# Row sums of the later modulations with the data as stationary operand, and the context norm's squares two steps earlier

## The chip, the cores and the metric

The kernel runs on one core of one Trainium2 chip. The metric is device time in microseconds (us) from one launch, the median over a few runs; lower is better. The core has five engines that run side by side and wait for each other by semaphores: TensorE (PE; its loads of stationary operands are listed apart as PEld), VectorE (DVE), ScalarE (ACT), GpSimd (POOL) and SyncE (SP), which here issues nearly all DMA transfers from one queue.

## The reference

One layer of a diffusion backbone over 1024 latent tokens and 256 context tokens, model width 1024, all in f32. Each sub-layer's input is normed and modulated by a shift and a scale, and its output scaled by a gate; these nine vectors ("modulations", m = 0 to 8) come from one product each for latents and context:

```
mod_lat = silu(c) @ w_mod + b_mod        # (1024) @ (1024 x 9*1024)
mod_ctx = silu(c_ctx) @ w_mod + b_mod
ml, mc = split(mod_lat, 9), split(mod_ctx, 9)
x  = x  + 0.5*ml[2]*swiglu(modulate(rms_norm(x,  norm1_g), ml[0], ml[1]), ffn1_w_in, ffn1_w_out)
cx = cx + 0.5*mc[2]*swiglu(modulate(rms_norm(cx, norm1_g), mc[0], mc[1]), ffn1_w_in, ffn1_w_out)
hx = modulate(rms_norm(x,  norm2_g), ml[3], ml[4])
hc = modulate(rms_norm(cx, norm2_g), mc[3], mc[4])
...  # hx, hc @ w_in: gated short convolution and grouped-query attention, merged
x = x + ml[5]*merge(...)
x = x + 0.5*ml[8]*swiglu(modulate(rms_norm(x, norm3_g), ml[6], ml[7]), ffn2_w_in, ffn2_w_out)
return rms_norm(x, final_g)
```

Context modulations above m = 4 are not needed, since the layer is the last.

## The kernel before

Activations lie transposed, channels on the 128 partitions and tokens along the free axis. PE's large products take each operand as two parts: a high part, the f32 number cast to a format that PE reads in one pass (`F32R`), and a low part, the difference (`split`: a cast on ACT, a subtraction on DVE). A product is three matmuls of parts. The FFN products (`Winograd`, `row_products`) use a fast scheme over 2 x 2 blocks with seven products instead of eight. Their inputs are loaded into `raw` tiles, added in part on POOL (`s`, `sum`), split into `wl` and fed to PE.

The first two modulations for the latents come from functions of their own at the start. All others are `later_mod`. It works in halves of 512 columns. For a half, eight tiles `rawm` (128 x 512) of `w_mod` are loaded, and DVE multiplies each by the 128 numbers of silu(c), one for each partition, and adds it into an accumulator `macc`, one accumulator for each stream (latents v = 0, context v = 1). What is left is a sum over the 128 partitions, for 512 columns, and it has to end with the 512 results laid out as 128 partitions x 4, in `modl` or `modc`, with the bias `bcol` added. The old way to do it is: split the accumulator into `acch` and `accl`; two matmuls with a column of ones (`ones_r`) as the stationary operand and 512 moving columns, which give one row of 512 sums in PSUM; a copy of the row on ACT that also reorders it (`mrow`); a DMA of 2 KB from that row into a 128 x 4 tile (`mcol`); an add on DVE.

There are 17 halves and 23 sums: three halves for the context alone (second half of m = 1, both of m = 0), six with both streams (m = 2, 3, 4), eight for the latents alone (m = 5 to 8).

`later_mod` is a generator. Each `yield` ends a step, and `run(steps, n)` in other loops takes n steps at a place, so that this work is issued between rounds of other products. A half takes 19 steps before: eight with a load and multiply-adds, four empty (`WAIT`), then the split and six steps, then the matmuls, copy, transfer and add, in step 19. Where steps are taken:

- First FFN, loop over 22 column blocks j: six steps at the end of each of j = 1 to 12 (`STEPS`), none at 13. Each of these j holds five to seven products of twelve matmuls. These 72 steps begin with the three context halves, then the first context norm `modulated_norm` (normc), then m = 2. After j = 13 come 14 rounds of context products with two steps each (`BATCH`), then 11 steps at the end of each j from 14 on. All that is left over is taken at once behind the loop.
- The mixing products, loop over i = 0 to 7: two steps of the second context norm (normc2) after a first group of seven products; from i = 3 on also eight steps of m = 5. One or two further groups follow in each i.
- The value projection over ten token tiles: three steps of m = 6 and 7 after each; then five after each group of heads. Here the weights are loaded four at a time (`by_four`).
- Second FFN: three steps of m = 8 after each j from 2 on.

`modulated_norm` for the 256 context tokens squares on ACT and adds on DVE (`sum_squares`, result `sq_acc`), ends the step, sums over the partitions on PE with `rstd_cols`, whose products already have the data stationary and the f32 column `ones` moving, computes 1/sqrt on DVE in eleven small operations (`rs_a`, `rs_y`, `rs_t`), waits four steps and then scales the channels, one in each step.

Order on the engines: the program is written for a scheduler that plans each engine's order from a model of costs. It may put instructions that it takes to be ready ahead of those issued earlier, except that one marked `pinned` stays behind the instruction issued just before it on its engine. Each engine then runs its list in order and waits at its head for whatever it needs. SP's queue does likewise: a transfer that waits for its data holds back every load behind it. Tiles come from pools with a fixed number of buffers: small working tiles (`ttile`: `rawm`, `macc`, `acch`, `accl`, `mrow`, `s1` to `s3`, `sq` and others) share eleven, and `ps_t` in PSUM has two.

Of the kernel before, what the change touches and what calls it, by code (L numbers as in the profile page):

```python
# [10 lines left out]
F32R = mybir.dt.float32r  # L11
# [7 lines left out]
P = 128  # L19
# [32 lines left out]
def tile_dit_layer(  # L52
# [44 lines left out]
    act, dve, pool, pe, sp = (Engine(e) for e in (nc.scalar, nc.vector, nc.gpsimd, nc.tensor, nc.sync))  # L97
# [11 lines left out]
    def uniq(s):  # L109
        n_tiles[0] += 1  # L110
        return f"{s}_{n_tiles[0]}"
# [4 lines left out]
    def ttile(name, n=512, dt=F32):  # L116
        t = tpool.tile([P, 512], dt, tag="t", name=uniq(name))
        return t[:, :n]

    def small(name, n, dt=F32):  # L120
        return spool.tile([P, n], dt, tag=f"s{n}_{name}", name=uniq(name))
# [4 lines left out]
    def ps_t(n=512):  # L126
        return psum.tile([P, 512], F32, tag="t", name=uniq("pt"), bufs=2)[:, :n]
# [4 lines left out]
    def matmul(out, w, x, start, stop, pinned=False, on=False):  # L132

        inst = pe.matmul(out, w, x, start=start, stop=stop, skip_group_check=on)
        if pinned:
            tc.keep_in_program_order(inst)
# [7 lines left out]
    def load(out, in_, pinned=False):  # L144
        inst = sp.dma_start(out=out, in_=in_)
        if pinned:
            tc.keep_in_program_order(inst)
# [4 lines left out]
    ones = const.tile([P, 1], F32, name="ones")  # L152
    dve.memset(ones[:], 1.0)
    ones_r = const.tile([P, 1], F32R, name="ones_r")
# [4 lines left out]
    bcol = const.tile([P, 72], F32, name="bcol")  # L159
# [26 lines left out]
    def col(name, k=0):  # L186
        o = voff[name] + k
        return cols[:, o : o + 1]
# [4 lines left out]
    modl = const.tile([P, 72], F32, name="modl")  # L193
    modc = const.tile([P, 40], F32, name="modc")


    def split(src, hi, lo, lo_eng=None, hi_eng=None):

        if hi_eng is dve:
            dve.tensor_copy(out=hi, in_=src)  # L200
        else:
            act.copy(out=hi, in_=src)
        (lo_eng or dve).tensor_sub(out=lo, in0=src, in1=hi.bitcast(F32))
# [47 lines left out]
    def rstd_cols(accs, n, dim):  # L251

        nt = n // P
        pss = ps_t(nt)
        for j in range(nt):
            for i, acc in enumerate(accs):
                matmul(
                    pss[:, j : j + 1], acc[:, j * P : (j + 1) * P], ones[:], start=(i == 0),
                    stop=(i == len(accs) - 1), pinned=True,
                )  # L260
        a = small("rs_a", nt)
        dve.tensor_scalar(out=a[:], in0=pss, scalar1=dim * EPS, scalar2=None, op0=ALU.add)
        return rsqrt_cols(a[:], nt)

    def bcast(y, n):

        pr = ps_t(n)
        for j in range(n // P):
            transpose(pr[:, j * P : (j + 1) * P], y[:, j : j + 1].to_broadcast([P, P]), pinned=True)
        return pr  # L270

    def later_mod(m, halves=(0, 1), streams=None, by_four=False):

        if streams is None:
            streams = (0, 1) if m < 5 else (0,)
        for half in halves:
            raws = fetch_mod(m, half, False) if by_four else None
            accs = [ttile(f"macc{v}") for v in streams]
            o = m * D + half * 512
            for k in range(KD):  # L280
                if by_four:
                    raw = raws[k // 2][:, k % 2]
                else:
                    raw = ttile("rawm")
                    load(out=raw, in_=w_mod[0, k * P : (k + 1) * P, o : o + 512])
                for acc, v in zip(accs, streams):
                    s = silu_c[:, v * 8 + k : v * 8 + k + 1]
                    if k == 0:
                        dve.tensor_scalar(out=acc, in0=raw, scalar1=s, scalar2=None, op0=ALU.mult)
                    else:  # L290
                        dve.scalar_tensor_tensor(out=acc, in0=raw, scalar=s, in1=acc, op0=ALU.mult, op1=ALU.add)
                yield
            for _ in range(WAIT):
                yield
            parts = []
            for acc in accs:
                ah, al = ttile("acch", dt=F32R), ttile("accl", dt=F32R)
                split(acc, ah, al)
                parts.append((ah, al))
            for _ in range(6):  # L300
                yield
            for (ah, al), v in zip(parts, streams):
                mod, pm = (modl, modc)[v], ps_t()
                matmul(pm[:1], ones_r[:], ah, start=True, stop=False, pinned=True)
                matmul(pm[:1], ones_r[:], al, start=False, stop=True, pinned=True)
                row = ttile("mrow")
                act.copy(
                    out=row[:1].rearrange("o (p j) -> o j p", j=4), in_=pm[:1].rearrange("o (j p) -> o j p", j=4)
                )
                mcol = small("mcol", 4)  # L310
                sp.dma_start(out=mcol[:], in_=row[:1])
                c0 = m * 8 + half * 4
                dve.tensor_add(out=mod[:, c0 : c0 + 4], in0=mcol[:], in1=bcol[:, c0 : c0 + 4])
            yield

    def fetch_mod(m, half, pinned=True):
        raws = []
        for kk in range(KD // 2):
            raw = atile("rawm", (P, 2, 512))
            o = m * D + half * 512  # L320
            load(raw[:], w_mod[0, kk * 256 : (kk + 1) * 256, o : o + 512].rearrange("(a p) n -> p a n", p=P), pinned)
            raws.append(raw)
        return raws
# [106 lines left out]
    def sum_squares(xs, ch):  # L430
        n = ch[2]
        acc, acc2 = ttile("sq_acc", n), ttile("sq_acc2", n)
        for k in range(KD):
            sq = (acc, acc2)[k] if k < 2 else ttile("sq", n)
            act.activation(out=sq, in_=xs(k, ch), func=AF.Square)
            if k >= 2:
                a = (acc, acc2)[k % 2]
                dve.tensor_add(out=a, in0=a, in1=sq)
        dve.tensor_add(out=acc, in0=acc, in1=acc2)
        return acc  # L440

    def modulated_norm(xs, hh, hl, ch, gain, mod, m):

        s, o, n = ch
        acc = sum_squares(xs, ch)
        yield
        y = rstd_cols([acc], n, D)
        for _ in range(WAIT):
            yield
        pr = bcast(y, n)  # L450
        for k in range(KD):
            if k:
                yield
            t = ttile("nt", n)
            dve.tensor_mul(out=t, in0=xs(k, ch), in1=pr)
            dve.tensor_scalar(
                out=t, in0=t, scalar1=gain[s][:, k : k + 1], scalar2=mod[s][:, m * 8 + k : m * 8 + k + 1],
                op0=ALU.mult, op1=ALU.add,
            )
            split(t, hh(k, ch), hl(k, ch))  # L460
        yield
# [613 lines left out]
    for k in range(4):  # L1075
        if k % 2:
            half1.shifted(h0[k][:, 0], k, xh[k])
        else:
            dve.tensor_scalar(
                out=h0[k][:, 0], in0=xh[k], scalar1=gain1["l"][:, k : k + 1], scalar2=modl[:, k : k + 1],  # L1080
# [3 lines left out]
    start = half1.start_by_half()  # L1084
# [44 lines left out]
    for i in range(2):  # L1129
        sp.dma_start(out=cxd[i], in_=xc.t[i][:].rearrange("p a b -> p (a b)"))  # L1130
    hc = Context("h1ch", F32R), Context("h1cl", F32R)
    normc = modulated_norm(xc, *hc, CC, gain1, mods, 0)

    def all_later_mods():
        yield from later_mod(1, (1,), (1,))
        yield from later_mod(0, (0, 1), (1,))
        part_gain(gain1["c"], 0, "g1", "c", 0, 8)
        for _ in normc:
            yield
        for m in range(2, 5):  # L1140
            yield from later_mod(m)
# [68 lines left out]
    for j in range(NH):  # L1210
        half1.side = side(j) if j >= SIDE_FROM else None
        u, c = half1.next_first()
        v, b = half1.second(u)
# [25 lines left out]
    for d in range(0, KD, 2):  # L1239
# [8 lines left out]
        for e in range(2):  # L1248
            te = t[:, e * CT : (e + 1) * CT]
            dve.scalar_tensor_tensor(  # L1250
                out=te, in0=pt[:, e * CT : (e + 1) * CT], scalar=gate1["c"][:, d + e : d + e + 1], in1=te, op0=ALU.mult, op1=ALU.add
# [78 lines left out]
    for i in range(KD):  # L1330
# [6 lines left out]
        for ch, bg, gc in mixed():  # L1337
            gate(gcd, i, ch, gc)
            o = ch[1]
            y = ttile("y")  # L1340
            dve.tensor_scalar(out=y, in0=u[:, o : o + 512], scalar1=col("w1", i), scalar2=None, op0=ALU.mult)
            for j in (0, 2):
# [3 lines left out]
                    out=ya, in0=u[:, a + j - 1 : b + j - 1], scalar=col(f"w{j}", i), in1=ya, op0=ALU.mult, op1=ALU.add  # L1346
# [42 lines left out]
    for kt in range(10):  # L1389
        ch = CC if kt < 2 else C0 if kt < 6 else C1  # L1390
        o = (kt if kt < 2 else (kt - 2) % 4) * P
# [327 lines left out]
    for ch in (C0, C1):  # L1719
        o = ch[1]  # L1720
        for d in range(KD):
# [7 lines left out]
                out=xs(d, ch), in0=ps, scalar=modl[:, 40 + d : 41 + d], in1=xs(d, ch), op0=ALU.mult, op1=ALU.add  # L1729
# [12 lines left out]
        out=gf[:], in0=cols[:, voff["gf"] : voff["gf"] + 8], scalar1=math.sqrt(D), scalar2=None, op0=ALU.mult  # L1742
# [46 lines left out]
    for j in range(NH):  # L1789
# [3 lines left out]
        v, b = fast.second(u)  # L1793
# [81 lines left out]
```

## Time and profile before

| | |
|---|---|
| median of three runs | 2670.65 us (2669.2 to 2675.72) |
| the profiled execution | 2670.08 us, span 2668.3 us |
| PE | busy 2633.8 us, 99% of the span |
| DVE | 2002.0 us, 75% |
| ACT | 1173.6 us, 44% |
| POOL | 558.4 us, 21% |
| mean granted PE clock | 0.996 |

The span runs from the first to the last instruction; the execution's own time has some 2 us around it. Matmuls overlap in PE's pipeline: a duration in a row is longer than the distance to the next start, so PE's price of an instruction is read from start to start. In a time line, a bracket at a row's end is the idle time of the engine before it and what ended that. In a table of stretches the columns are the length, the busy time of each engine asked for with its number of instructions, the granted PE clock, the DMA share and GB/s. The row of a tile gives the shortest, median and longest duration in ns. All matmul and vector lines carry the line number 90, that of the helper which issues them, so tiles tell the groups apart.

### The profile page before, as it was taken

Reading aid. Unit: us, or ns where it says so; the run is one execution under the profiler, and the core shown is the slowest. Engines: PE = TensorE matmul, PEld = TensorE weight load, DVE = VectorE, ACT = ScalarE, POOL = GpSimd, SP = SyncE. Lnnn points to the kernel's source line nnn. Section 1 sums busy time; section 2 is a strip of 40 time slices with the busy share of each in tenths; the row PEclk is TensorE's granted clock in tenths of the full one; section 3 lists DMA queues with packets and bytes.
Section 4 is the critical chain, followed back from the end, with each engine's and each line's share of the span. In section 5 each row is a group of like instructions: output and inputs, shape, how many; then the busy total and the mean of one; then the engine's idle time right before and its main releaser. Section 6 shows DMA issues by size and latency. Waiting matters only on the chain.

```text
span 2668.3 us, 36840 instructions
## 1 busy us (share of the span) xinstructions
PE 2633.8 (99%) x13373; PEld 2220.0 (83%) x13373; DVE 2002.0 (75%) x3356; ACT 1173.6 (44%) x2317; POOL 558.4 (21%) x449
## 2 busy tenths in 40 slices
PE   8999999999999999999999999999999999999998
PEld 6787799888778878888999888888888888888888
DVE  5788976788887899877598676685458976657885
ACT  6532454333454643333355576574236333334443
POOL 0134301111020034332033122141001532330200
PEclk9999999999999999999999999999999999999999
DMA  8566475345984355342522432113525643227841
GB/s 320 194 194 189 138 230 158 115 131 187 302 206 119 126 179 173 98 134 72 202 68 92 91 95 62 35 41 98 167 87 171 196 146 97 86 88 285 188 90 64
DMA packets 371471, 381.12 MB, mean 143 GB/s; under 512 B 19526, under 2 KB 258264, under 8 KB 371288
## 3 DMA queue, kind: packets, MB, share of 16 engines
q1 hardware_dynamic: 360472, 357.22, 41.4%
q0 software_dynamic: 10816, 21.53, 4.9%
q8 instruction: 105, 1.72, 0.3%
q14 instruction: 78, 0.64, 0.1%
HBM read 308.88 MB, written 69.76 MB: 142 GB/s over the span
## 4 chain that ended last, share of the span: by engine, by line
PE 90%; DVE 5%; DMA 2%; issue 1%; ACT 1%; POOL 1%; SPq 0%; DVEq 0%; POOLq 0%; ACTq 0%
PE ps L90 74%; PE po L90 8%; PE pt L90 8%; DVE wl L90 1%; DVE r L90 1%; DMA raw<-in_ffn_w_in_dram 1%; DVE nt L90 0%; DMA rawm<-in_w_mod_dram 0%; DMA ws<-in_ffn_w_out_dram 0%; DVE u L90 0%; DVE macc L90 0%; POOL s L90 0%; DVE y L90 0%; POOL sum L90 0%; DVE sq_acc L90 0%
## 5 line engine op out<-in xcount | busy, mean ns | idle before, releaser
L90 PE MATMUL ps<-r,wl 128*128 128x512 f32 x5196 | 1206.8, 391 | 9.6 <-DVE wl L90 3.1
L90 PEld LDWEIGHTS ps<-r,wl 128*128 128x128 f32 x5196 | 974.4, 189 | 218.8 <-DVE wl L90 5.9
L90 ACT CAST wl<-raw 128x512 fp32r<-128x512 f32 x287 | 177.7, 620 | 229.8 <-PE ps L90 173.3
L90 DVE TENSOR_TENSOR wl<-raw,wl 128x512 fp32r<-128x512 f32 x287 | 202.3, 706 | 60.6 <-ACT wl L90 56.7
L90 ACT CAST wl<-sum 128x512 fp32r<-128x512 f32 x168 | 103.2, 620 | 231.9 <-PE ps L90 184.9
L90 DVE TENSOR_TENSOR wl<-sum,wl 128x512 fp32r<-128x512 f32 x168 | 152.2, 908 | 17.8 <-ACT wl L90 16.8
L90 POOL TENSOR_TENSOR sum<-raw 128x512 f32<-128x512 f32 x42 | 60.6, 1443 | 497.9 <-DMA raw<-in_w_in_dram 203.2
L90 DVE SCALAR_TENSOR_TENSOR macc<-rawm,silu_c,macc 128x512 f32<-128x512 f32 x178 | 148.0, 849 | 13.5 <-DMA rawm<-in_w_mod_dram 12.8
L90 DVE TENSOR_TENSOR u<-u,ps 128x512 f32<-128x512 f32 x186 | 126.2, 680 | 33.6 <-PE ps L90 33.6
L90 PE MATMUL ps<-wh,r 128*128 128x256 f32 x768 | 141.6, 284 | 0.0
L90 DVE TENSOR_TENSOR pts<-pt,pts 128x512 fp32r<-128x512 f32 x160 | 108.7, 687 | 41.1 <-ACT pts L90 39.3
L90 ACT CAST pts<-pt 128x512 fp32r<-128x512 f32 x160 | 93.3, 595 | 86.4 <-PE pt L90 82.7
L90 DVE TENSOR_REDUCE m<-ps 128x1 f32<-128x512 f32 (+1 forms) x192 | 110.3, 595 | 23.9 <-PE ps L90 22.3
L90 ACT CAST rh<-hid 128x512 fp32r<-128x512 f32 x132 | 81.3, 620 | 104.6 <-PE ps L90 91.6
L90 PE MATMUL ps<-rh,wl 128*128 128x512 f32 x360 | 122.0, 389 | 0.0
L90 PEld LDWEIGHTS ps<-wh,r 128*128 128x128 f32 x768 | 120.8, 192 | 0.7 <-issue 0.6
L90 POOL TENSOR_TENSOR sum<-raw,sum 128x512 f32<-128x512 f32 x42 | 62.0, 1476 | 268.7 <-DVE wl L90 261.8
L90 ACT CAST wh<-raw 128x512 fp32r<-128x512 f32 (+1 forms) x85 | 67.9, 801 | 103.2 <-PE ps L90 70.2
L90 POOL TENSOR_TENSOR s<-raw 128x512 f32<-128x512 f32 x22 | 32.0, 1457 | 378.5 <-DMA raw<-in_ffn_w_in_dram 297.1
L90 PE MATMUL po<-pts,vh 128*128 128x512 f32 x256 | 110.0, 435 | 0.2 <-ACT pts L90 0.2
L90 PE MATMUL ps<-wl,r 128*128 128x256 f32 x384 | 109.0, 284 | 0.0
L90 DVE TENSOR_TENSOR rl<-hid,rh 128x512 fp32r<-128x512 f32 x132 | 90.3, 686 | 21.7 <-PE ps L90 11.7
(317 smaller groups left out, 5382.9 us busy)
## 6 DMA issues: line engine op xcount, KB each, us to landing
raw<-in_ffn_w_in_dram SPq DMA_DIRECT2D x130, 512.0 KB
raw<-in_ffn_w_out_dram SPq DMA_DIRECT2D x72, 512.0 KB
raw<-in_w_in_dram SPq DMA_DIRECT2D x61, 512.0 KB
rawm<-in_w_mod_dram SPq DMA_DIRECT2D x104, 256.0 KB
hid<-hd SPq DMA_DIRECT2D x40, 512.0 KB
rawm<-in_w_mod_dram SPq DMA_DIRECT2D x32, 512.0 KB
ws<-in_ffn_w_out_dram POOLq DMA_DIRECT2D x30, 512.0 KB, 6.5
ucd<-uc SPq DMA_DIRECT2D x29, 512.0 KB
```

Source lines behind the costliest of these rows:

```text
L90: inst = getattr(self.engine, name)(*args, **kw)
```

## The change

In `later_mod` the split, the two matmuls over 512 columns, the row copy and the transfer go. Each accumulator, as it is (f32), becomes the stationary operand in four products of 128 x 128, with the f32 column `ones` moving. Each gives 128 sums, one on each partition, in one column of a PSUM tile `pm`; both streams share one tile. DVE adds the bias from PSUM into `modl` or `modc`. The sum is issued in step 13 of a half, right after the four empty steps, and four steps follow: a half has 16 steps. In `modulated_norm` the sum of squares is followed by three step ends instead of one.

```diff
             for _ in range(WAIT):
                 yield
-            parts = []
-            for acc in accs:
-                ah, al = ttile("acch", dt=F32R), ttile("accl", dt=F32R)
-                split(acc, ah, al)
-                parts.append((ah, al))
-            for _ in range(6):
+            pm = ps_t(4 * len(streams))
+            for i, acc in enumerate(accs):
+                for j in range(4):
+                    matmul(
+                        pm[:, 4 * i + j : 4 * i + j + 1], acc[:, j * P : (j + 1) * P], ones[:], start=True, stop=True,
+                        pinned=True,
+                    )
+            c0 = m * 8 + half * 4
+            for i, v in enumerate(streams):
+                dve.tensor_add(
+                    out=(modl, modc)[v][:, c0 : c0 + 4], in0=pm[:, 4 * i : 4 * i + 4], in1=bcol[:, c0 : c0 + 4]
+                )
+            for _ in range(4):
                 yield
-            for (ah, al), v in zip(parts, streams):
-                mod, pm = (modl, modc)[v], ps_t()
-                matmul(pm[:1], ones_r[:], ah, start=True, stop=False, pinned=True)
-                matmul(pm[:1], ones_r[:], al, start=False, stop=True, pinned=True)
-                row = ttile("mrow")
-                act.copy(
-                    out=row[:1].rearrange("o (p j) -> o j p", j=4), in_=pm[:1].rearrange("o (j p) -> o j p", j=4)
-                )
-                mcol = small("mcol", 4)
-                sp.dma_start(out=mcol[:], in_=row[:1])
-                c0 = m * 8 + half * 4
-                dve.tensor_add(out=mod[:, c0 : c0 + 4], in0=mcol[:], in1=bcol[:, c0 : c0 + 4])
-            yield
...
         acc = sum_squares(xs, ch)
-        yield
+        for _ in range(3):
+            yield
         y = rstd_cols([acc], n, D)
```

## The prediction

> **What bounds the kernel now.** I read the page first (busy shares, then the chain that ended last), then the tiles of the sums that the change touches, then the time line of TensorE (PE) around them, and last the waits and the clock.
>
> ```profile
> span 2668.3 us, 36840 instructions
> ...
> PE 2633.8 (99%) x13373; PEld 2220.0 (83%) x13373; DVE 2002.0 (75%) x3356; ACT 1173.6 (44%) x2317; POOL 558.4 (21%) x449
> ...
> PE 90%; DVE 5%; DMA 2%; issue 1%; ACT 1%; POOL 1%; SPq 0%; DVEq 0%; POOLq 0%; ACTq 0%
> ```
>
> PE is busy for 99% of the span and carries 90% of the chain. So each microsecond put into PE's stream lengthens the program nearly one for one, and what other engines save is worth only the PE idle time that it ends. The stretches in which the later modulations run show how little of that there is:
>
> ```profile
> 200.00:270.00 70.00, 66.72 (x285) 1.00 0.59 183
> ...
> 330.00:690.00 360.00, 360.00 (x2088) 1.00 0.54 176
> ```
> ```profile
> 1330.00:1460.00 130.00, 130.00 (x1039) 127.03 (x1038) 114.24 (x299) 64.14 (x218) 41.79 (x80) 1.00 0.23 74
> 2080.00:2300.00 220.00, 220.00 (x972) 181.71 (x971) 163.10 (x221) 70.47 (x116) 80.90 (x56) 1.00 0.44 135
> ```
>
> The columns are length, then PE busy. PE is idle for 3.3 us between 200 and 270, and for nothing from 330 to 690, from 1330 to 1460 and from 2080 to 2300, where 19 of the 23 sums are.
>
> **The sums on PE, old and new.** The rows of the old sums and of the row-sum products that already have the new form (f32 data stationary, a column of ones moving):
>
> ```profile
> L90 PE MATMUL pt<-acch,ones_r x23: 388/397/400, 192.6 to 2280.6; 128*1 128x512 f32 x23
> ...
> L90 PE MATMUL pt<-accl,ones_r x23: 389/397/398, 192.9 to 2280.8; 128*1 128x512 f32 x23
> ```
> ```profile
> L90 PE MATMUL pt<-ones,sq x104: 168/250/250, 876.8 to 2660.2; 128*128 128x1 f32 x104
> ...
> L90 PE MATMUL pt<-ones,sq_acc x40: 164/250/250, 294.7 to 2019.1; 128*128 128x1 f32 x40
> ```
>
> There are 23 sums, of two matmuls each. The code asks for 52 products on sq and 20 on sq_acc, and the trace has 104 and 40: an f32 product is two instructions, each with a stationary load of its own. So 4 products for each of 23 sums are 184 instructions in place of 46. Durations overlap, so the price is read from start to start:
>
> ```profile
> 192.64 0.40 PE L90 MATMUL pt<-acch,ones_r 128*1 128x512 f32 x1
> 192.87 0.40 PE L90 MATMUL pt<-accl,ones_r 128*1 128x512 f32 x1
> 193.11 7.22 PE L90 MATMUL ps<-r,wl 128*128 128x512 f32 x31
> ```
> ```profile
> 2017.69 0.28 PE L90 MATMUL pt<-ones,sq_acc 128*128 128x1 f32 x2
> ...
> 2019.16 0.36 PE L90 MATMUL pt<-ones,sq 128*128 128x1 f32 x2
> 2019.39 4.84 PE L90 MATMUL ps<-r,wl 128*128 128x512 f32 x20
> ```
>
> Old sum: 193.11 - 192.64 = 0.47 us. New form: 16 instructions from 2017.69 to 2019.39 are 1.70 us, and the 20 matmuls behind them take 4.84 where 19 x 0.227 + 0.39 would be 4.70 (0.227 is the step of back-to-back 512-column matmuls: 31 in 7.22 us is 30 steps and one duration of 0.40), so about 0.1 more; 1.80 for 16, 0.90 for one sum of 8. The moving side shrank from 512 columns to one, but the 128 x 128 stationary load now sets the step of 0.112 us. Cost: 23 x (0.90 - 0.47) = **+9.9 us**. The nearest other block, four instructions in 0.44 us (294.75 to 295.19, below), makes it 0.88 and +9.4: the term is narrow.
>
> [...]
>
> **What is removed elsewhere.** Per sum one cast and one row copy on ScalarE (ACT), one subtraction on VectorE (DVE) and one small transfer on SP:
>
> ```profile
> L90 ACT CAST acch<-macc x26: 602/619/623, 23.2 to 2237.8; 128x512 fp32r<-128x512 f32 x26
> L90 DVE TENSOR_TENSOR accl<-macc,acch x26: 675/684/694, 23.9 to 2239.2; 128x512 fp32r<-128x512 f32 x26
> ...
> L90 ACT COPY mrow<-pt x23: 1056/1077/1127, 193.4 to 2281.3; 1x512 f32<-1x512 f32 x23
> ```
> ```profile
> SPq L90 <- ACT mrow L90: 57.8, 4, 17.2
> ```
>
> 23 x (0.62 + 1.08) = 39 us of ACT, 23 x 0.68 = 16 us of DVE, and 58 us in which SP's queue stood behind a waiting column transfer, the next modulation's loads and weight loads behind it. By itself all of it is worth nothing: PE has no idle time beside it in the rows above. The cover is PE's stream; were PE idle there, up to the 16 us of DVE would count. The column adds (0.16 us) stay and read PSUM; the three tiles fewer per sum ease the pool of 11 and can only bring loads forward. The two places where PE does wait:
>
> **The first context norm.** DVE's queue stood behind the column transfer, and the squares' sum for the norm was queued behind that add:
>
> ```profile
> 284.46 0.75 DVE L90 TENSOR_TENSOR sq_acc<-sq_acc,sq 128x256 f32<-128x256 f32 x2
> 288.78 0.16 DVE L90 TENSOR_TENSOR modc<-mcol,bcol 128x4 f32<-128x4 f32 x1 [3.58 <-DMA mcol<-mrow]
> ...
> 293.71 0.89 DVE L90 TENSOR_TENSOR sq_acc<-sq_acc,sq_acc 128x256 f32<-128x256 f32 x1
> ```
> ```profile
> 289.83 3.11 PE L90 MATMUL ps<-r,wl 128*128 128x512 f32 x13
> 294.75 0.58 PE L90 MATMUL pt<-ones,sq_acc 128*128 128x1 f32 x4 [1.81 <-DVE sq_acc L90]
> 295.19 7.10 PE L90 MATMUL ps<-r,wl 128*128 128x512 f32 x23
> ```
> ```profile
> 292.00:296.00 4.00, 2.19 (x13) 1.59 (x12) 4.00 (x5) 1.47 (x3) 3.67 (x3) 1.00 0.17 65
> 296.00:300.00 4.00, 4.00 (x12) 3.13 (x11) 4.00 (x6) 1.53 (x3) 1.66 (x1) 0.57 0.32 104
> ```
>
> DVE idled 3.6 us for the transfer; PE's product on the squares came 2.0 us late start to start (13 steps of 0.227 after 289.83 is 292.78, it began at 294.75), and behind that gap the granted clock was 0.57 over 4 us: another 4 x 0.43 = 1.7 us. After the change that add waits for PE alone, so the 3.6 us of DVE idling are gone, more than the 2.0 that PE lost. I take -3.7, the ends being 0 and -3.7. [...]
>
> The second edit does nothing at this place. Steps are taken six at a time here, after a whole round of products; three halves of 19 steps put squares and product at steps 58 and 59 (the call of 55 to 60), three of 16 at steps 49 and 52 (the call of 49 to 54). No PE work is issued between them either way.
>
> **The second context norm.** Here two steps are taken per column group, so the product and the eleven small DVE operations behind it move from the first group (about 980 to 1003) to the second. DVE is full there and PE waits for it at the end:
>
> ```profile
> 1010.81 4.70 PE L90 MATMUL ps<-r,wl 128*128 128x512 f32 x20
> 1017.02 3.26 PE L90 MATMUL ps<-r,wl 128*128 128x512 f32 x13 [1.51 <-DVE wl L90]
> ```
> ```profile
> 985.00:1017.00 32.00, 30.51 (x134) 24.70 (x132) 31.90 (x51) 8.44 (x16) 13.11 (x9) 1.00 0.52 163
> ```
>
> DVE is busy 31.9 of 32 us. Eleven operations less before 1017 can end the wait of 1.5 us, or pass it on; ends -1.5 and 0, I take half: -0.8. The norm then ends one group later (15 steps of the 16 taken) and its first reader is behind two more groups: nothing.
>
> **New waits.** The sum now waits for the last multiply-add itself, five steps on, where it used to be eleven, with the cast between. Where the steps come six or eight to a call after a round of products, a round lies between. In two halves (the first of modulations 3 and 4: 11 steps per call, products at the call's first three or two steps, the sum at its eighth or seventh) nothing does; the planner can put later products ahead there, PE is full from 330 to 690, and I take 0 (ends 0 and 3.7 each, the price at 294). At modulation 6, steps come three per token tile:
>
> ```profile
> 1296.25 0.49 DVE L90 TENSOR_SCALAR macc<-rawm,silu_c 128x512 f32<-128x512 f32 x1 [2.23 <-DMA rawm<-in_w_mod_dram]
> ...
> 1301.15 1.53 DVE L90 SCALAR_TENSOR_TENSOR macc<-rawm,silu_c,macc 128x512 f32<-128x512 f32 x2
> ```
> ```profile
> 1287.23 0.28 PE L90 MATMUL ps<-wh,h2ch 128*128 128x256 f32 x1
> ...
> 1292.98 0.28 PE L90 MATMUL ps<-wh,r 128*128 128x256 f32 x1
> ```
>
> Two tiles take 5.75 us, so the fifth, behind which step 13 falls, ends at 1287.23 + 5 x 2.875 = 1301.6; the last multiply-add ended at 1301.15 + 1.53 = 1302.7. PE would wait 1.1 us: taken, with ends 0 and 3.3 (the loads another 2.2 late). In the first three halves loads land late too (idle 3.3 us, 200 to 270). Six multiply-adds instead of five are bunched in one call, three tiles fewer are held: I take 0, ends -3.3 and +3.7.
>
> **Sum.** +9.9 - 3.7 - 0.8 + 1.1 = +6.5 us on the profiled execution's own 2670.08: 2676.6. The median of the runs, 2670.65, is 0.6 above it: 2677. A difference under 0.3% (8 us) is about what a measurement of this kernel cannot tell from none, so the forecast is no change that can be told, on the slow side: between 2662.6 and 2678.7.
>
> **Rivals.**
> *The idle time goes as well.* PE pays the 9.4, and the waits of 200 to 270, 294 and 1017 all end: 9.4 - 3.7 - 1.5 - 3.3 = +0.9, 2671.5. For it: the loads behind them are held up by tiles and a queue that the change frees. Against: they wait chiefly for transfers that stay.
> *The sum waits for the multiply-add.* One further wait like that at 294 in the early or the bunched halves, with its clock, is 3.7: 6.5 + 3.7 is 2681; two, 2684.5. It decides from 1.5 us on. For it: DVE is behind on loads at 200 to 270 and at 1296; against: a round of products lies between in most halves.
> *The other side: hidden stationary loads.* Were the loads hidden behind 512-column matmuls, each instruction would cost only what the first of the block above does: the first two take 0.13 (2017.69 to 2017.82), the second of them the usual 0.112, so the first some 0.02. 184 x 0.025 = 4.6, less 10.8 is -6.2, with the other terms -9.6: 2661, faster. It decides below 0.033 us each. Against it: the block's remaining steps are 0.112, and the matmul behind pays for the first. [...]
> [...]
>
> **Chances.** Forecast 0.5 (2672 to 2682), idle time gone too 0.22, new waits 0.2, hidden loads 0.04, four per product 0.02, a reshuffle of the order elsewhere 0.02. Slower by over 0.3% (from 2678.7): the new waits, the four, and the upper third of the forecast's case: 0.38. Faster: 0.05. Within: 0.57. The range 2668 to 2685 leaves out part of the new waits and the two far cases.
>
> **What would show it.** Right: 184 instructions on ones and macc, PE count 13373 + 138, each eight taking 0.9 us; no column transfer and no PE gap before the first norm's product, no half clock near 300; the wait at 1017 shorter. Wrong: waits of PE for macc of more than 1 us each, a half clock behind them, or steps of those products far from 0.112 us.

## The result and the profile after

The changed kernel takes 2678.68 us (median of 19 runs, 2675.2 to 2684.28) beside 2671.49 for the kernel before (19 runs, 2668.54 to 2680.99): ratio 1.0025, 95% interval [1.0017, 1.0032]. The whole interval lies above 1, so the change is slower, by 7.2 us at the median. That is inside the 0.3% which the forecast called no change, on the slow side, and the interval's upper end just passes it. The profiled execution took 2676.07 us against 2670.08, so +6.0.

The page of the changed kernel, its first lines:

```profile
span 2674.2 us, 37004 instructions
...
PE 2641.8 (99%) x13511; PEld 2237.1 (84%) x13511; DVE 1981.1 (74%) x3333; ACT 1141.2 (43%) x2271; POOL 564.2 (21%) x449
```

PE has 13373 + 138 matmuls. ACT lost 32 us of work and DVE 21, and the program is longer all the same. The group of the new products, and one sum in the time line of PE:

```profile
L90 PE MATMUL pt<-ones,macc x184: 164/250/250, 177.9 to 2229.7; 128*128 128x1 f32 x184
```
```profile
206.06 0.95 PE L90 MATMUL pt<-ones,macc 128*128 128x1 f32 x8
206.86 8.47 PE L90 MATMUL ps<-r,wl 128*128 128x512 f32 x36
```

Eight instructions take 0.80 us to the next start, and the 36 matmuls behind them 8.47 where 35 steps of 0.227 and one duration of 0.39 are 8.34, so about 0.1 more: 0.9 for a sum, as computed. The 184 instructions stand in 13 blocks of eight and five of sixteen (0.90 and 1.80 us), 20.7 us, in place of 23 x 0.47 = 10.8: +9.9. For the whole program I added up PE's start-to-start steps at full clock, waits left out: 2590.3 us before, 2600.1 after, +9.8. This sum is good to about 1 us, since the usual length of each step goes into it.

So PE's own stream grew by 9.8 and the span by 5.9. What came back lies in the stretch of the three early halves and the first context norm. The tables of stretches, before and after (length, PE busy with its number of instructions, granted clock, DMA share, GB/s):

```profile
270.00:340.00 70.00, 68.19 (x328) 0.98 0.47 147
```
```profile
200.00:270.00 70.00, 70.00 (x318) 1.00 0.61 194
270.00:340.00 70.00, 67.14 (x345) 1.00 0.53 166
```

With the row of 200 to 270 shown in the prediction (66.72), PE is busy for 134.91 of these 140 us before and 137.14 after: 2.2 us less waiting. The clock of 0.98 is 1.00 now: another 70 x 0.02 = 1.4, in which the half clock behind 294 (1.7) shows. The time line after:

```profile
270.30 0.50 PE L90 MATMUL pt<-ones,sq_acc 128*128 128x1 f32 x4
...
291.54 21.67 PE L90 MATMUL ps<-r,wl 128*128 128x512 f32 x94 [0.53 <-ACT wl L90]
314.13 3.00 PE L90 MATMUL ps<-r,wl 128*128 128x512 f32 x12 [0.93 <-DVE u L90]
318.53 8.45 PE L90 MATMUL ps<-r,wl 128*128 128x512 f32 x36 [1.39 <-ACT u L90]
...
1017.58 12.79 PE L90 MATMUL ps<-r,wl 128*128 128x512 f32 x48 [2.04 <-DVE wl L90]
```
```profile
1019.00:1023.00 4.00, 4.00 (x13) 0.63 0.53 195
```

The norm's product runs at 270.30 without a wait, where it ran at 294.75 behind 1.81 us. The 3.3 us of waits before 270 are gone too, and three new waits behind the product, 2.9 us together, take part of it back. The wait at 1017 did not shrink: 1.51 us became 2.04, and now a half clock follows (0.63 over 4 us: 1.5 us lost). No wait of PE for `macc` is in the trace.

### The profile page after: what moved, and what is told of

Its sections match the earlier page's. It is cut to its first block, busy times and chain, and to the rows that moved or that the text cites. A ratio compares the mean times of both kernels' runs of the same rounds, so it can differ in the third digit from the quotient of the medians.

```text
span 2674.2 us, 37004 instructions
## 1 busy us (share of the span) xinstructions
PE 2641.8 (99%) x13511; PEld 2237.1 (84%) x13511; DVE 1981.1 (74%) x3333; ACT 1141.2 (43%) x2271; POOL 564.2 (21%) x449
## 4 chain that ended last, share of the span: by engine, by line
PE 60%; DVE 2%; ACT 0%; issue 0%; DMA 0%; POOL 0%; DVEq 0%; ACTq 0%; POOLq 0%
PE ps L90 50%; PE pt L90 5%; PE po L90 5%; DVE wl L90 0%; DVE r L90 0%; DVE y L90 0%; DMA raw<-in_ffn_w_in_dram 0%; DVE u L90 0%; DVE rs_t L90 0%; DVE nt L90 0%; POOL sum L90 0%; ACT pts L90 0%; DVE v L90 0%; DVE pts L90 0%; DVE rs_y L90 0%
```

## Experiments

Times and ratios are against runs of the kernel before on the same chip. In the time lines a bracket is idle time and what ended it. "Nominal" is the sum of PE's steps at full clock, as above.

**The second edit undone.** In the kernel after, one step end behind the sum of squares instead of three:

```diff
-        for _ in range(3):
-            yield
+        yield
```

> The new sum with the norm's old single step. Price theory (the new form costs 0.43 us of PE for each of 23 sums, +9.9 us, of which the wait behind the column transfer gives back some): as the changed kernel, +5 to +9 us on before; the wait of PE near 1017 is back at the first kernel's 1.5 us or below the changed kernel's 2.0. If the second edit is what costs: within 2 us of before.

2688.87 us, ratio 1.0055 [1.0039, 1.0071]; nominal 2600.1. The stretches, PE's waits, and the row of ACT behind the first of them:

```profile
200.00:270.00 70.00, 70.00 (x318) 1.00 0.63 195
270.00:340.00 70.00, 62.87 (x291) 0.98 0.46 146
```
```profile
281.28 2.38 PE L90 MATMUL ps<-r,wl 128*128 128x512 f32 x8 [2.91 <-ACT wl L90]
...
299.16 0.73 PE L90 MATMUL ps<-r,wl 128*128 128x512 f32 x2 [2.93 <-ACT wl L90]
```
```profile
279.79 0.40 ACT L90 CAST h1ch<-nt 128x256 fp32r<-128x256 f32 x1 [11.30 <-DVE nt L90]
...
280.63 1.12 ACT L90 CAST wl<-s 128x512 fp32r<-128x512 f32 x2
```

The prediction said that the second edit does nothing at the first norm. It does much there: without it the first cast of a scaled channel stands at the head of ACT's queue for 11.3 us, with the casts of the next products' inputs behind it, and PE is idle for 7.1 us of 270 to 340. The edit puts not only the squares' product but every later step of the norm two steps on, into another call; I had placed squares and product in their calls and stopped there. The first scaled channel comes four steps behind the product, and the calls end at steps 54, 60 and 66. Squares, product and first channel are steps 58, 59 and 63 in the kernel before, 49, 52 and 56 after the change, and 49, 50 and 54 here. Of the three, only here does the channel fall into the product's own call; in the two others its first cast waits 1.59 and 4.82 us on ACT.

The profiled execution is the fastest of the six. It has 4.3 us more idle time in these 140 us than the change; the rest of the distance between the medians is not in it.

**The second edit alone.** The kernel before with the three step ends in the norm:

```diff
-        yield
+        for _ in range(3):
+            yield
```

> Old sums, only the two further step ends in the context norm. Price theory: -2 to +2 us, with the wait of 1.8 us before the first norm's product still there (squares and product stay in one call of six steps) and the DVE add still waiting for the column transfer. If the second edit were what removes the first norm's wait: that wait is gone and the time is some 3.7 us lower.

2677.15 us, 1.0013 [1.0003, 1.0024]; nominal 2590.3. PE's wait at the norm:

```profile
311.35 0.66 PE L90 MATMUL pt<-ident,rs_y 128*128 128x128 f32 x2 [2.74 <-DVE rs_y L90]
```

With the old sums the edit loses a little: the wait at 294 goes, but the norm's transposes wait 2.74 us for 1/sqrt. Neither expectation holds: the wait was to stay, or else the time was to fall with it. In steps, squares, product and first channel are 58, 61 and 65 here, and the channel is again in the product's call, 61 to 66. The edit's sign depends on how many steps a half has, since that decides in which call each step of the norm falls.

**The second edit at the first norm only.** The kernel after, with one step end again at the second norm:

```diff
-        for _ in range(3):
+        for _ in range(3 if m == 0 else 1):
             yield
```

> The changed kernel with the three step ends behind the sum of squares at the first context norm only (m = 0); the second norm (m = 3) has one again, as before. Theory (all that the second edit is worth lies at the first norm): the time is that of the changed kernel within 2 us, 2675 to 2681; no wait of 2.9 us on ScalarE's casts at 281 and 299 as in the kernel with the new sums alone; waits of 200 to 345 us stay at 3 to 4 us; and at the second norm the wait near 1017 goes from 2.0 back to about 1.5 us with the last small operation of the norm 1 to 2 us earlier on VectorE. Rival (the prediction's step: the second norm's later product takes eleven small VectorE operations from the stretch before 1017): undoing it lengthens the wait at 1017 to over 2 us, +0.8 to +2 us. Second rival (the gain of the second edit over the new sums alone, 8 us, comes from the second norm or from the order elsewhere): 2684 to 2689 us.

2679.69 us, 1.0021 [1.0013, 1.003]: that of the changed kernel. So all that the second edit is worth beside the new sums lies at the first norm. The early waits are 4.6 us in this profile, where 3 to 4 were expected. At the second norm:

```profile
1019.95 3.01 PE L90 MATMUL ps<-r,wl 128*128 128x512 f32 x12 [0.47 <-DVE wl L90]
1025.02 15.26 PE L90 MATMUL ps<-r,wl 128*128 128x512 f32 x59 [2.05 <-DVE wl L90]
```

The wait there (2.05 us, in a program that is some 7 us later by then) is neither shorter nor longer: both numbers that had been expected of it, 1.5 us and well over 2, miss. The last wait of this stretch is 1.55 us in the kernel with the second edit undone everywhere, and 0.99 and 0.88 in two kernels below, so half a microsecond here cannot be put down to the norm's steps.

**The new sum at the old step.** One step end in the norm, and the new products in step 19 of 19:

```diff
+            for _ in range(6):
+                yield
             pm = ps_t(4 * len(streams))
...
-            for _ in range(4):
-                yield
+            yield
...
-        for _ in range(3):
-            yield
+        yield
```

> The new sum at its old place: step 19 of 19, with the norm's old single step, so that only the form of the sum differs from before. Price theory: +5 to +10 us, each eight products 0.90 us start to start, no product waits for macc, and no wait of DVE for a column transfer at the first norm. Re-planning theory (what costs is the shorter half of 16 steps and what it bunches): within 2 us of before.

2678.99 us, 1.0018 [1.0009, 1.0028]; nominal 2600.2.

```profile
200.00:270.00 70.00, 69.28 (x308) 1.00 0.64 199
270.00:340.00 70.00, 70.00 (x362) 1.00 0.53 167
```

This is the change of the sum with all other work in its old steps, and PE's early waits nearly vanish (0.7 us of 140, before 5.1). So the early gain is the removed work's and tiles', not the norm's place; what is left of the loss is again PE's 9.8.

**The old sum in 16 steps.** The kernel before, with three step ends instead of six behind the split:

```diff
-            for _ in range(6):
+            for _ in range(3):
                 yield
             for (ah, al), v in zip(parts, streams):
```

> The old sum (two matmuls over 512 columns, row copy, transfer) in halves of 16 steps: three of the six steps behind the split are taken out. Price theory: -3 to +3 us, since PE's work is unchanged; the sums stay at 0.47 us. Re-planning theory: +5 us or more, with waits of PE at the places where the changed kernel has them (near 291, 314 and 318).

2679.26 us, 1.0024 [1.0012, 1.0035]; nominal 2590.1.

```profile
200.00:270.00 70.00, 65.85 (x282) 1.00 0.61 191
270.00:340.00 70.00, 63.49 (x269) 0.98 0.48 151
```

No product was added, and yet it is as slow as the change: 10.7 us idle in these 140, twice as much as before. Squares, product and first channel are again steps 49, 50 and 54, and the channel's first cast on ACT waits 9.68 us. The count of steps alone is worth as much as the 184 products, and 16 is the worse count for one step end in the norm, with old sums and with new.

**The transfer put back.** The kernel after, with a copy of the four columns on ACT, a DMA of the same size into the 128 x 4 tile, and the add behind it. No working tile of the eleven is used:

```diff
-                dve.tensor_add(
-                    out=(modl, modc)[v][:, c0 : c0 + 4], in0=pm[:, 4 * i : 4 * i + 4], in1=bcol[:, c0 : c0 + 4]
-                )
+                mrow, mcol = small("mrow", 4), small("mcol", 4)
+                act.copy(out=mrow[:], in_=pm[:, 4 * i : 4 * i + 4])
+                sp.dma_start(out=mcol[:], in_=mrow[:])
+                dve.tensor_add(out=(modl, modc)[v][:, c0 : c0 + 4], in0=mcol[:], in1=bcol[:, c0 : c0 + 4])
```

> The changed kernel with the small transfer put back: the sums go from PSUM to a tile of 128 x 4 on ACT, by DMA to another, and then into the add on DVE. Transfer theory (DVE's queue behind that transfer is what made PE wait at the first context norm): a wait of PE of 1 us or more returns between 260 and 330, DVE waits 2 us or more for the transfer there, and the time is 2 to 6 us above the changed kernel. If the fewer tiles or the order are what removed that wait: within 2 us of the changed kernel, no such wait.

2682.26 us, 1.0038 [1.0025, 1.005]: the interval overlaps that of the change, [1.0017, 1.0032], so a small cost of the transfer is not told from none.

```profile
200.00:270.00 70.00, 69.46 (x312) 1.00 0.60 187
270.00:340.00 70.00, 66.89 (x332) 1.00 0.54 173
```

PE's busy time there, 136.35 us, is within 0.8 of the 137.14 without it. SP's queue stands behind such transfers for 73 us in this kernel and for 58 in the one before, and in these 140 us that costs PE next to nothing. DVE waits for them at 217 and 260 (1.99 and 1.50 us), both some microseconds ahead of the norm's sum of squares; a transfer that stands before that sum, as at 288 in the kernel before, is not tried by this run.

**The add that waits for the column, on POOL.** The kernel before with `pool.tensor_add` in place of `dve.tensor_add` for that add, so that DVE's queue holds nothing that waits for the transfer:

```diff
-                dve.tensor_add(out=mod[:, c0 : c0 + 4], in0=mcol[:], in1=bcol[:, c0 : c0 + 4])
+                pool.tensor_add(out=mod[:, c0 : c0 + 4], in0=mcol[:], in1=bcol[:, c0 : c0 + 4])
```

> The kernel before with one word changed: the add behind the column transfer runs on POOL, so that DVE's queue no longer waits for the transfer. Transfer theory: the wait of 1.8 us before the first norm's product and the half clock behind it go, -2 to -4 us on before. Rival (tiles and loads cause it): the wait stays, or PE waits elsewhere in 200 to 340, within 2 us of before; POOL's own sums for the weights come later and can add up to 3 us.

2675.86 us, 1.0013 [1.0004, 1.0021]. ACT and PE at the first norm:

```profile
289.53 1.03 ACT L90 ACTIVATE sq<-xc 128x256 f32<-128x256 f32 x3 [3.92 <-DMA mcol<-mrow]
```
```profile
295.70 0.58 PE L90 MATMUL pt<-ones,sq_acc 128*128 128x1 f32 x4 [2.04 <-DVE sq_acc L90]
```

The wait stays, 2.04 us. So DVE's queue behind the transfer, the prediction's cause, is not what holds the norm by itself. The squares on ACT wait for the same transfer, and so they did before:

```profile
288.84 1.03 ACT L90 ACTIVATE sq<-xc 128x256 f32<-128x256 f32 x3 [3.85 <-DMA mcol<-mrow]
```

A square reads nothing of the sum's. What it needs is a free working tile, and the row `mrow` held one of the eleven until the DMA had read it.

**The row in a tile of the big pool.** The kernel before, only this tile moved:

```diff
-                row = ttile("mrow")
+                row = atile("mrow")[:, :512]
```

> The kernel before with one edit: the row of 512 sums (mrow), which the column transfer reads, lies in a tile of the big pool instead of one of the eleven small working tiles. Sums, steps, transfers and the add are as before. Theory (the wait at the first context norm comes from ScalarE's squares, which waited 3.9 us for the transfer to give back the working tile that held the row): no square waits for the column transfer any more, the 1.8 to 2.0 us wait of TensorE before the norm's product near 294 goes and its half clock with it, -2 to -3.7 us; other waits of 200 to 345 us (6.2 us before) get no longer. Rival (the transfer itself, at the head of SP's queue or ahead of the add in VectorE's, holds the norm): the wait at 294 stays at 1.8 to 2.2 us, and the time is that of before within 1 us. A second rival: the tile is not what counts, the planner only shuffles the order; then waits of 200 to 345 come out anywhere from 2 to 9 us.

2689.03 us, 1.0056 [1.0042, 1.0071]; nominal 2590.4.

```profile
291.82 0.58 PE L90 MATMUL pt<-ones,sq_acc 128*128 128x1 f32 x4 [1.09 <-DVE sq_acc L90]
...
700.84 0.79 PE L90 MATMUL ps<-rh,wl 128*128 128x512 f32 x1 [3.22 <-ACT wl L90]
...
722.02 0.80 PE L90 MATMUL pt<-rh,wl 128*128 128x512 f32 x1 [4.41 <-ACT wl L90]
```

At the norm it went the theory's way in part: no square waits for the column any more, the wait is 1.09 instead of 1.81 and no half clock follows. What is left has the prediction's own cause in view. DVE's add still waits for the column, and the next addition of squares stands right behind it:

```profile
288.86 0.16 DVE L90 TENSOR_TENSOR modc<-mcol,bcol 128x4 f32<-128x4 f32 x1 [1.47 <-DMA mcol<-mrow]
288.94 0.43 DVE L90 TENSOR_TENSOR sq_acc<-sq_acc,sq 128x256 f32<-128x256 f32 x1
```

So one transfer held the norm in two ways at once in the kernel before, ACT through the row's tile and DVE through its queue, and taking away one leaves the other. Both edits together were not run. The time of the whole is far off the theory, and the reason is at 640 to 720. The same stretches before, and with the row moved:

```profile
640.00:660.00 20.00, 20.00 (x105) 1.00 0.86 300
660.00:680.00 20.00, 20.00 (x105) 1.00 1.04 391
```
```profile
640.00:660.00 20.00, 20.00 (x107) 1.00 0.50 159
660.00:680.00 20.00, 17.45 (x88) 0.99 0.49 164
680.00:700.00 20.00, 17.62 (x74) 0.92 1.05 402
700.00:720.00 20.00, 16.78 (x60) 0.83 1.05 406
```

From 660 to 700 the DMA engines are full before (share 1.0). Here they carry half as much from 640 to 680, are full 20 us later, and PE waits for what lands late, with half clocks on top. Fewer transfers under way while the row holds a big tile fit that; which of them it held back was not tried.

**The old sum with its tiles out of the eleven.** The kernel before; the two parts in one tile of the big pool, the row copied back over the accumulator. A second version does so only for m below 3 and leaves the later parts in the working tiles:

```diff
-                ah, al = ttile("acch", dt=F32R), ttile("accl", dt=F32R)
-                split(acc, ah, al)
-                parts.append((ah, al))
+                w = atile("accs", (P, 2, 512), F32R)
+                split(acc, w[:, 0], w[:, 1])
+                parts.append((w[:, 0], w[:, 1], acc))
...
-            for (ah, al), v in zip(parts, streams):
+            for (ah, al, row), v in zip(parts, streams):
...
-                row = ttile("mrow")
```

> The kernel before with fewer of the eleven working tiles held: the parts of the accumulator go into one tile of the large pool, and the row is copied into the accumulator's own tile, so a sum holds one working tile for each stream where it held three in turn. Tile theory (the loads in 200 to 340 come late because tiles are held): PE's idle time between 200 and 270, 3.3 us before, falls below 1.5, and the time is 2 to 6 us below before. If the transfer and DVE's queue are the cause: within 2 us of before, the wait at the first norm still there.

2669.17 us, 0.9987 [0.9978, 0.9995]: faster than the kernel before by a hair; nominal 2590.3.

```profile
200.00:270.00 70.00, 68.71 (x299) 1.00 0.62 191
270.00:340.00 70.00, 69.86 (x361) 1.00 0.53 172
...
708.22 0.80 PE L90 MATMUL pt<-rh,wl 128*128 128x512 f32 x1 [6.12 <-ACT wl L90]
```

The old sum, with its products, copy and transfer all there, has the early waits down to 1.4 us of 140. So the sums' working tiles, and the order that the planner makes with them, are what cost PE time here; the runs do not keep these two apart. The row's tile is not the chief one: with it alone moved, above, 4.2 us of the 140 are idle. But 6.12 us come back at 708, in the stretch where the DMA engines are full. The version with big tiles for m below 3 only:

> The old sum with the row copied back into the accumulator's own tile throughout; the two parts lie in one tile of the big pool for the halves of m = 0, 1 and 2 only (the first FFN's early columns), and in the small working tiles from m = 3 on. Theory (the gain of the lean form comes from the early halves, 200 to 345 us, where it cut TensorE's waits from 6.2 to 2.1 us, and its own new wait of 6.3 us at 708 comes from tiles of the big pool that m = 3 and 4 hold): early waits stay near 2 us, the wait at 708 is back to the 0.4 to 1.2 us of before, 2662 to 2667 us. Rival (the wait at 708 comes from the row being held in the accumulator's tile, or from a different order of the loads altogether): it stays at 4 to 6 us, 2667 to 2670 us.

2670.64 us, 0.999 [0.9982, 0.9998].

```profile
200.00:270.00 70.00, 69.02 (x298) 1.00 0.61 187
270.00:340.00 70.00, 69.63 (x356) 1.00 0.53 171
...
707.70 0.50 PE L90 MATMUL pt<-rh,wl 128*128 128x512 f32 x1 [1.52 <-ACT wl L90]
```

The early waits came as expected and the wait at 707 nearly (1.52 us for 0.4 to 1.2), yet the time is that of the first version, above the 2662 to 2667 expected: the intervals overlap almost wholly. The profiled spans are equal too (2667.4), with 60.2 us of waits beside 61.7 and 5.6 us lost to half clocks beside 4.2: most of the wait that left 708 turned up in smaller ones elsewhere. I can name no single place for it.

**The sum without its four empty steps.** The kernel after, the sum in the step of the last multiply-adds, the four steps behind it:

```diff
-            for _ in range(WAIT):
-                yield
             pm = ps_t(4 * len(streams))
...
-            for _ in range(4):
+            for _ in range(4 + WAIT):
                 yield
```

> The changed kernel with the sum issued in the same step as the last multiply-adds, instead of four empty steps later; the four steps follow the sum, so a half still takes 16 steps. Theory (the sum is late enough by the planner's own order: it put products ahead of the sum where the multiply-add was not due, so no wait on the accumulator was seen): TensorE's waits on macc stay under 2 us in all, 2674 to 2680 us, the nominal TensorE time 2600 as in the changed kernel. Rival of the prediction (the sum waits for the multiply-add where no round of products lies between): a wait of 1 to 3.7 us in many of the 17 halves, 2685 to 2710 us, which would say that the four empty steps are what kept it from showing.

2679.41 us, 1.0025 [1.0012, 1.0038], the ratio of the change. PE waits nowhere for `macc`, even so. The prediction's rival of a sum that waits for the multiply-add is not borne out: the order planned for PE puts other products ahead of a sum that is not due (modulation 6, below).

**Each product twice.** The kernel after; each group of four is issued two times and writes the same columns again:

```diff
-            for i, acc in enumerate(accs):
+            for i, acc in [*enumerate(accs)] * 2:
                 for j in range(4):
```

> The changed kernel with each of the four products of a sum issued twice (the same result written again). Price theory: 184 more instructions at 0.112 us, +20.7 us on the changed kernel, +27 on before, give or take 5 for waits that move. If the stationary loads were hidden: +4.6 on the changed kernel.

2704.43 us, 1.0126 [1.0111, 1.0141]; nominal 2620.8: 20.7 us for 184 more instructions in 23 sums, 0.90 each. The full step of 0.112 us is paid each time, so the rival of hidden loads falls. The rest of the difference to 2678.68, some 5 us, goes with the clock, 0.994 instead of 0.996 in the profiled executions:

```profile
346.00:352.00 6.00, 6.00 (x46) 1.00 0.04 10
352.00:356.00 4.00, 4.00 (x23) 0.57 0.13 35
```
```profile
348.01 3.63 PE L90 MATMUL pt<-ones,macc 128*128 128x1 f32 x32
```

PE has no gap there; the half clock comes behind 3.5 us of one-column products. Behind two more of the five blocks of 32, at 421 and 629, the granted clock is 0.57 over 4 us as well (424 to 428 and 632 to 636).

## Why the prediction was right

The forecast was +6.5 on the profiled execution, 2676.6; it took 2676.07, and the median moved by 7.2 to 2678.68. The terms:

| term | forecast | in the trace |
|---|---|---|
| 23 sums on PE | +9.9 | +9.8 |
| first norm, with 200 to 270 | -3.7 | -2.2 idle, -1.7 half clock |
| second norm | -0.8 | +0.5 idle, +1.5 half clock |
| modulation 6 | +1.1 | 0 |
| elsewhere | 0 | about -2.0 |

Idle and clock together gave back 3.9 us of 9.8 (waits over the whole span 60.0 to 57.0, half clocks 6.8 to 5.8); the last row is what these leave. That the sum comes within 1 us is luck in part: the second norm is off by 2.8 us to one side, modulation 6 and the rest of the program by 3.1 to the other, and a profile shows the half clocks of one execution.

- **The sums: right, to 0.1 us**, and shown by doubling them. The start-to-start price of a neighbouring row was enough. No run shows four instructions per product: the 184 for 92 products are two each. The weight loads keep the same step: in the trace before two loads of the block at 2018 start every 0.22 us (2018.02, 2018.24, 2018.46, 2018.69). The 0.025 us in the rival of hidden loads is the distance of the first two products of that block, 2017.686 to 2017.711.
- **The first norm: right in size, half right in its cause, and wrong on the second edit.** The step "after the change that add waits for PE alone, so the 3.6 us of DVE idling are gone" named DVE's queue alone. With the add on POOL the wait stayed, since ACT's squares waited for the same transfer through the row's working tile; with that tile moved ACT's wait and 0.7 us of PE's went, and DVE's queue was what was left in the way. The sentence on three tiles fewer that "can only bring loads forward" had a further gain in it and the sum priced it at nothing: the 3.3 us idle from 200 to 270 are all gone, and 2 of them go with the old sum too when its tiles lie elsewhere. The three new waits of 2.9 us, not in the sum either, take most of that back. "The second edit does nothing at this place" failed most: without it the change costs 1.0055 instead of 1.0025. These errors met in a number that fits.
- **The second norm: no gain.** The step was that eleven small DVE operations leave the stretch before 1017. The norm's product did move, from 982 to 992.5. The operations did not leave the stretch: they end at about 1004 both ways, well ahead of 1017, and from 985 to 1017 DVE is busy for 31.76 of 32 us after, 31.90 before. The last of them, before and after:

```profile
1002.91 0.73 DVE L90 SCALAR_TENSOR_TENSOR rs_y<-rs_t,rs_y 128x2 f32<-128x2 f32 x1
```
```profile
1004.65 0.16 DVE L90 SCALAR_TENSOR_TENSOR rs_y<-rs_t,rs_y 128x2 f32<-128x2 f32 x1
```

- **Modulation 6: no wait.** After, PE's first product of the projection and the first sum of m = 6:

```profile
1290.29 0.28 PE L90 MATMUL ps<-wh,h2ch 128*128 128x256 f32 x1
...
1307.33 0.95 PE L90 MATMUL pt<-ones,macc 128*128 128x1 f32 x8
```

The sum stands 17.04 us behind the projection's start, where the prediction counted five tiles, 14.4; the last multiply-add had ended 0.6 us ahead of it. I had put it where its step falls in the program; in the kernel without the empty steps it is issued earlier and stands at 17.04 us too (1291.80 to 1308.84). The planner's order decides.

- **Elsewhere:** the waits of 1.23 and 0.43 us at 711 and 713 are gone, and the half clocks fall elsewhere: of the three in the first 100 us before, one is left, and there are new ones at 769 and 1019. These fall differently from run to run: the 19 runs of the change have mean clocks of 0.994 to 0.997, and go from 2684.28 us (0.994) to 2675.2 (0.997). With 0.001 of the clock worth 2.7 us (an estimate, 0.001 of the span of 2674.2), most of that spread of 9 us is the clock.

## What to carry to other kernels

Where PE is full, price an exchange by the start-to-start time on PE alone: here 53 us less work on ACT and DVE, and 58 us less standing still in a queue, were worth less than 0.43 us per sum on PE. When a change frees engines, tiles and a queue at once, give each back by itself: here it was the shared working tiles that had cost time, and the old sum with its tiles elsewhere keeps the early gain without the new products. And when steps of a schedule are counted anew, follow all the steps behind the edit into their calls, not only the one that the edit names: three steps fewer in a half, which put a norm's first reader into the call of its product, cost as much as 184 products.

## What the runs showed of the hardware that was not expected

- The half clocks of the two traces, as measured: before, the granted clock is 0.50 for 3.41 us from 30.14, 64.28, 91.58, 296.38 and 958.57 us, which are 10, 8, 60 and 194 times 3.4133 us apart; after, it is 0.50 for as long from 32.11, 769.38, 960.53 and 1018.56 us, which are 216, 56 and 17 times 3.4133 apart. One more reaches into the last 10 us of each.
- Waits of nearly the same length differed in what followed. After, PE waits 1.90 us at 769, and the granted clock is 0.50 from 769.38 on. Before, it waits 1.93 us ahead of the same product, at 771, and the clock is 1.00 from 767 to 777. What sets the two apart was not shown. The rows of PE and the stretches, after and then before:

```profile
768.75 0.50 PE L90 MATMUL ps<-rl,wl 128*128 128x512 f32 x1 [1.90 <-DVE rl L90]
```
```profile
765.96:769.38 3.42, 1.52 (x7) 1.00 0.82 152
769.38:772.79 3.41, 3.41 (x10) 0.50 0.22 29
```
```profile
771.10 0.50 PE L90 MATMUL ps<-rl,wl 128*128 128x512 f32 x1 [1.93 <-DVE rl L90]
```
```profile
767.00:777.00 10.00, 8.07 (x36) 1.00 0.66 134
```

- A half clock also came where PE had no gap. With each product issued twice, PE is busy for all 6.00 us from 346 to 352, 3.5 of them with the block of 32 one-column products from 348.01, and the clock over the next 4 us is 0.57. Behind the five blocks of 16 in the trace after, 1.70 us each to the next start, none came: the clock is 1.00 from 340 to 640.
